# Triangular substitution four columns at a time, and group norms in one stream

## The chip, the cores and the metric

The program runs on one core of a Trainium2 chip. The metric is device time in microseconds (us) of one execution, the median of three. A core has a matrix engine (TensorE, in the views PE, with its weight loads PEld), three engines for elementwise work (VectorE = DVE, ScalarE = ACT, GpSimd = POOL), a queue engine (SyncE = SP) and DMA engines. Every engine runs its own instructions in program order and waits on semaphores for the others.

## What is computed

One layer of a bidirectional backbone on 1024 latent and 128 context tokens, in fp32, model width 1024. The projection w_in feeds two mixers, an RWKV-7 scan in both directions (16 heads of 64) and a gated short convolution; then come the projections w_pa and w_pb, the gated merge, w_o, and a convolutional FFN. Cut to what matters here:

```python
def step(s, inp):                       # the recurrent scan, per direction and head
    r_t, w_t, k_t, v_t, a_t, b_t = inp
    sa = jnp.einsum('bhij,bhj->bhi', s, a_t)
    s = s * w_t[:, :, None, :] + sa[..., None] * b_t[:, :, None, :] + v_t[..., None] * k_t[:, :, None, :]
    return s, jnp.einsum('bhij,bhj->bhi', s, r_t)
...
y = y_f + y_b                           # group norm per head, bonus, gate
o = yn * lp['gn_w'] + lp['gn_b'] + (bonus_f + bonus_b)
...
merged = g_a * (o_a @ lp['w_pa']) + g_b * (o_b @ lp['w_pb'])
x = x + gt1 * (merged @ lp['w_o'])
```

## The kernel before

**Tiles.** The 1152 tokens are processed in three thirds of 384. A dense matrix product runs over weight tiles of 128 output channels; each third takes eight blocks of 128 input channels, and each block three fp32r matmuls (high and low parts of weight and operand), all into the PSUM tile psd. These are the dense matmuls; their operand names the stage: `psd<-h` is w_in, `psd<-x` w_pb and w_pa, `psd<-g` and `psd<-a` the later ones. A weight arrives as wraw by POOL's DMA queue and is split into whi (ACT) and wlo (POOL or DVE).

**The scan in items.** The recurrence is done in chunks of 128 tokens. There are 36 items: four groups of four heads (pp 0 to 3) by nine chunks (n 0 to 8, the last for context), both directions in one item. An item needs *prep* (per pair of heads and third: decays and rates, the matmuls lps), *prep2* (Gram products gpk and gpb on PE, masked into the tiles G, E and O on DVE), the inversion of unit triangular matrices, and the *scan* proper (small matmuls px and py, with DVE work on Wt and Mp between them). After the chunks with n of at least 4 a *finish* runs: group norm, bonus and gate (matmuls fps, six DVE steps for each pair of heads), and a store to OA.

**The inversion.** The 32x32 diagonal blocks are inverted by substitution on DVE (`chain`, L1301 to L1323): Dm holds on each partition the entries of one block, X eight rows of its inverse. For each of 31 columns there is one multiply (`Xt<-X,Dm`) and one add (`X<-X,Xt`), 62 DVE instructions, each dependent on the one before, after each pair a yield. Then four DMAs (`Xd<-X`, ACT's queue) and four more (`G<-Xd`, SP's) bring the blocks back, and `merge` (L1325) joins them with PE (mps).

**The order.** A planner writes the order while the program is built. A clock `clk.now` advances by a fixed cost for each matmul; VectorE, ScalarE and GpSimd have modelled end times. A stream is a generator; it may go on when its own time has come, its condition holds and, where it has a gate, the modelled backlog of DVE and ACT is below it. `drive` alternates one dense matmul with all streams that may go on. The streams of the scan (`start`, L1019) are scan_all, merge_all, vfill_all, prep2_all, load_all, chain_all and prep_all, plus one stream for each finish. So a modelled cost moves the instructions of every engine, and a dense matmul stands between scan work wherever the model has the scan waiting.

**Stages.** While w_in and then w_pb run densely, the streams do the scan beside them. w_pb takes its operand x from OB, split in DVE and ACT instructions at its beginning. Then w_pa takes OA, which every finish must have written; its operand reuses the memory of the scan, as do the 64 wx instructions (L396, 128x1024, the modulation's dot products), placed from the scan's end on. The evacuations are `pbz` for w_pb and `paz`, `mg` for w_pa. w_o and the FFN follow.

Of the kernel before, what the change touches and what calls it, by code (L numbers as in the profile page):

```python
# [8 lines left out]
F32 = mybir.dt.float32  # L9
F32R = mybir.dt.float32r  # L10
AF = mybir.ActivationFunctionType
ALU = mybir.AluOpType
# [3 lines left out]
P = 128  # L16
# [30 lines left out]
class Clock:  # L47


    def __init__(self):  # L50
        self.now = 0.0
        self.e = {"V": 0.0, "A": 0.0, "G": 0.0}
# [24 lines left out]
class Kern:  # L77
# [9 lines left out]
    def mm(self, out, lhsT, rhs, start, stop, cost):  # L87
        self.clk.now += cost
        return self.nc.tensor.matmul(out, lhsT=lhsT, rhs=rhs, start=start, stop=stop)  # L89
# [894 lines left out]
class Scan:  # L984
# [4 lines left out]
    def __init__(self, K, const, apool, par, pc, mask, ident, bones, x0, hw0, hka, oka, dr):  # L989
        self.K, self.nc, self.pc, self.dr = K, K.nc, pc, dr  # L990
        self.mask, self.ident, self.bones, self.x0 = mask, ident, bones, x0
        self.hw0, self.hka, self.oka = hw0, hka, oka
        self.eps = const.tile([P, 1], F32, name="gneps", tag="gneps")
        K.nc.gpsimd.memset(self.eps, GN_EPS)
        self.psx = apool("psx", 1, PSUM)
        self.psy = apool("psy", 1, PSUM)
        self.psm = apool("psm", 3, PSUM)
        self.sets = apool("sets", 3)
        self.one = apool("one", 1)
        self.two = apool("two", 2)  # L1000
        self.ys = apool("ys", 4)
        self.fin = apool("fin", 1)
        self.drp = apool("drp", 2, DRAM)
        nc = K.nc
        self.reset = self.one.tile([P, TH], F32, name="reset", tag="reset")
        nc.gpsimd.memset(self.reset, 1.0)
        nc.gpsimd.memset(self.reset.rearrange("p (c t) -> p c t", t=C)[:, :, 0:1], 0.0)
        self.e65 = self.one.tile([P, 6, C + 1], F32, name="e65", tag="e65")
        nc.gpsimd.memset(self.e65[:, :, 0:1], 1.0)
        self.lwl = self.one.tile([P, 4, P], F32R, name="lwlo", tag="lwlo")  # L1010
        nc.gpsimd.memset(self.lwl[64:128].bitcast(F32), 0.0)
        self.items = [(pp, n) for pp in range(4) for n in range(9)]
        self.info = {}

        self.W = self.one.tile([P, 2, 4, 2, C], F32, name="Wt", tag="Wt")
        self.y, self.PC = {}, {}
        self.NY = 4

    def start(self):  # L1019
        K = self.K  # L1020
# [55 lines left out]
        def scan_all(s):  # L1076
            for i, (pp, n) in enumerate(self.items):
                yield lambda: ("merge", i) in ev and ("prep2", i) in ev
                yield from self.scan(s, i, pp, n)
                ev.add(("scan", i))  # L1080
                if n >= 4:
                    key = 7 - n if n < 8 else 8
                    K.spawn(lambda s2, pp=pp, key=key: self.finish(s2, pp, key), 4, gate=1000, ahead=0)

        K.spawn(scan_all, 0, ahead=0)
        K.spawn(merge_all, 0.5, ahead=0)
        K.spawn(vfill_all, 0.7, ahead=600)
# [213 lines left out]
    def chain(self, s, i):  # L1301


        K = self.K
        inf = self.info[i]
        X, Dm = inf["X"], inf["Dm"]
        tmp = self.one.tile([P, 8, 32], F32, name="Xt", tag="Xt", bufs=2)
        Dv = Dm.rearrange("p (u t) -> p u t", t=32)
        for u in range(31):
            m, n = u // 4 + 1, 31 - u  # L1310
            t_, x_ = tmp[:, 0:m, 0:n], X[:, 0:m, u + 1:32]
            K.tt(s, t_, X[:, 0:m, u:u + 1].to_broadcast([P, m, n]), Dv[:, u:u + 1, u + 1:32].to_broadcast([P, m, n]),
                 ALU.mult)
            K.tt(s, x_, x_, t_, ALU.add)
            s.t = K.clk.e["V"]
            yield
        Xd = self.drp.tile([32, 8, 4, 32], F32, name="Xd", tag="Xd", bufs=4)
        for g in range(4):
            K.dma(Xd[:, :, g, :], X[32 * g:32 * g + 32], "Xw")
        for rb in range(4):  # L1320
            blk = rb % 2
            K.dma(inf["G"][32 * rb:32 * rb + 32, :, 32 * blk:32 * blk + 32],
                  Xd[rb * 8:rb * 8 + 8].rearrange("e m g t -> (m g) e t"), "Xr")  # L1323
# [209 lines left out]
```

## Time and profile before

| | us |
|---|---|
| median of 3 runs | 2983.45 (2982.43 to 2989.89) |
| the profiled execution | 2987.0 |
| its span, first to last instruction | 2985.1 |
| TensorE busy | 2769.4 (93%) |
| VectorE busy | 2012.6 (67%) |
| ScalarE busy | 1267.4 (42%) |
| GpSimd busy | 494.4 (17%) |

Read it so: TensorE is the engine nearest to the span, and its share is an average over stages. From about 330 to 1028 us w_in runs beside preps and the first items; from 1063 to 1740 us w_in runs beside 23 items, one behind another; w_pb runs from 1813 to 1927 us, w_pa to about 2027 us, and the rest is w_o and the FFN. An idle microsecond of an engine costs time only where the end of the program waits for it.

### The profile page before, as it was taken

What the parts mean: (1) busy time and instruction counts of PE and PEld (TensorE: products, weight loads), DVE (VectorE), ACT (ScalarE), POOL (GpSimd) and SP (SyncE); (2) the same over time, 40 slices, a digit from 0 to 9 for tenths busy, and PEclk for the clock granted to TensorE, in tenths of its full rate; (3) what the DMA queues carried; (4) which work ended last, traced back from release to release, by engine and by line L of the source; (5) the groups of instructions that cost most, each with busy time, mean ns of one, the idle gap of its engine ahead of it and who ended that gap; (6) DMA issues with size and microseconds to landing.
All of it is one profiled execution on the core that took longest, in us unless ns stands there. A gap on an engine that the chain in (4) does not pass through costs nothing. (4 is left out here: it accounts for less than half of the span.)

```text
span 2985.1 us, 63295 instructions
## 1 busy us (share of the span) xinstructions
PE 2769.4 (93%) x24762; PEld 2514.1 (84%) x24762; DVE 2012.6 (67%) x5039; ACT 1267.4 (42%) x2544; POOL 494.4 (17%) x678
## 2 busy tenths in 40 slices
PE   7896998999989999889999998999999999999997
PEld 3884887878778777777777788899999999999996
DVE  7457785687667689888887857955555454555556
ACT  4474645555454634334543454123443241424243
POOL 3211121121221111111111112200001101010101
PEclk9997999999999999999999999999999999999998
DMA  4577646466565645545554538843211111111112
GB/s 195 163 238 224 199 148 194 154 175 183 156 185 145 216 109 126 131 109 134 140 139 108 136 115 311 264 141 98 65 43 36 50 40 46 41 41 43 40 44 80
DMA packets 402641, 388.49 MB, mean 130 GB/s; under 512 B 189478, under 2 KB 354214, under 8 KB 402342
## 3 DMA queue, kind: packets, MB, share of 16 engines
q1 hardware_dynamic: 331174, 280.08, 31.1%
q0 software_dynamic: 32000, 99.65, 11.0%
q10 hardware_dynamic: 39168, 4.73, 1.1%
q8 instruction: 195, 3.19, 0.5%
q14 instruction: 104, 0.84, 0.1%
HBM read 268.17 MB, written 116.13 MB: 129 GB/s over the span
## 5 line engine op out<-in xcount | busy, mean ns | idle before, releaser
L89 PE MATMUL psd<-h,whi 128*128 128x384 f32 x3216 | 907.7, 353 | 17.2 <-ACT h L105 9.3
L89 PEld LDWEIGHTS psd<-h,whi 128*128 128x128 f32 x3216 | 591.8, 192 | 52.6 <-issue 12.6
L89 PE MATMUL psd<-h,wlo 128*128 128x384 f32 x1608 | 564.9, 351 | 1.3 <-POOL wlo L110 1.3
L89 PE MATMUL psd<-g,whi 128*128 128x384 f32 (+1 forms) x2112 | 543.2, 338 | 0.0
L105 ACT ACTIVATE whi<-wraw 128x512 fp32r<-128x512 f32 (+2 forms) x334 | 198.3, 594 | 494.3 <-PE psd L89 431.4
L89 PEld LDWEIGHTS psd<-g,whi 128*128 128x128 f32 x2112 | 383.5, 188 | 0.3
L110 POOL TENSOR_TENSOR wlo<-wraw,whi 128x512 fp32r<-128x512 f32 x148 | 199.7, 1350 | 1098.6 <-ACT whi L105 950.9
L89 PE MATMUL psd<-g,wlo 128*128 128x384 f32 (+1 forms) x1056 | 355.9, 337 | 0.0
L89 PEld LDWEIGHTS psd<-h,wlo 128*128 128x128 f32 x1608 | 309.0, 192 | 14.5 <-issue 5.3
L110 DVE TENSOR_TENSOR Xt<-X,Dm 128x60 f32<-128x60 f32 (+24 forms) x1116 | 258.8, 234 | 28.7 <-DMA Dm<-Dd 1.1
L110 DVE TENSOR_TENSOR X<-X,Xt 128x60 f32<-128x60 f32 (+24 forms) x1116 | 253.0, 229 | 27.4 <-DMA O<-fa 0.3
L89 PE MATMUL psd<-a,whi 128*128 128x384 f32 x864 | 218.9, 334 | 0.0
L89 PE MATMUL psd<-x,whi 128*128 128x384 f32 x768 | 200.2, 341 | 10.4 <-ACT x L105 6.7
L89 PEld LDWEIGHTS psd<-g,wlo 128*128 128x128 f32 x1056 | 199.3, 189 | 0.0
L110 DVE TENSOR_TENSOR wlo<-wraw,whi 128x512 fp32r<-128x512 f32 (+2 forms) x186 | 113.7, 611 | 110.6 <-ACT whi L105 110.6
L89 PEld LDWEIGHTS psd<-a,whi 128*128 128x128 f32 x864 | 156.0, 188 | 0.0
L110 DVE TENSOR_TENSOR fu<-psd,rs 128x384 f32<-128x384 f32 x132 | 73.4, 556 | 117.6 <-PE psd L89 105.1
L89 PEld LDWEIGHTS psd<-x,whi 128*128 128x128 f32 x768 | 140.9, 191 | 13.1 <-ACT x L105 7.0
L89 PE MATMUL psd<-a,wlo 128*128 128x384 f32 x432 | 144.0, 334 | 0.0
L122 DVE SCALAR_TENSOR_TENSOR x<-psd,mod,x 128x384 f32<-128x384 f32 (+3 forms) x160 | 79.1, 514 | 94.0 <-PE psd L89 93.9
L105 ACT ACTIVATE BK<-BK,PC 128x128 f32<-128x128 f32 x288 | 94.4, 391 | 108.1 <-PE gpk L89 86.2
L89 PE MATMUL psd<-x,wlo 128*128 128x384 f32 x384 | 130.4, 340 | 4.4 <-DVE wlo L110 4.4
(213 smaller groups left out, 5111.6 us busy)
## 6 DMA issues: line engine op xcount, KB each, us to landing
wraw<-in_w_in POOLq DMA_DIRECT2D x134, 256.0 KB, 3.5
wraw<-in_w_up POOLq DMA_DIRECT2D x88, 256.0 KB, 2.9
llo<-lo SPq DMA_DIRECT2D x98, 192.0 KB, 3.0
BK<-fb SPq DMA_DIRECT2D x36, 512.0 KB, 5.0
Dm<-Dd POOLq DMA_DIRECT2D x144, 128.0 KB, 3.6
wx<-in_wmb SPq DMA_DIRECT2D x32, 512.0 KB, 5.3
fa<-fa SPq DMA_DIRECT2D x40, 384.0 KB, 2.7
fb<-ak SPq DMA_DIRECT2D x40, 384.0 KB, 3.2
```

Of the source, the lines that this page charges most:

```text
L89: return self.nc.tensor.matmul(out, lhsT=lhsT, rhs=rhs, start=start, stop=stop)
L105: self.nc.scalar.activation(out, in_, func, bias=bias, scale=scale)
L110: e.tensor_tensor(out, a, b, op)
L122: self.nc.vector.scalar_tensor_tensor(out, a, sc, b, op0, op1)
```

## The change

In `chain` the columns go four at a time. First the eight 4x4 blocks on the diagonal of each 32x32 block are inverted together into T4 (a copy, a memset, and two pairs of multiply and add). Then for each of the eight groups of four columns the finished columns are multiplied by Dm, and the result by T4. Such a product is one multiply (`Xt<-X,Dm` or `Xt<-X,T4`) into a tile of rows by four columns by terms, and one reduce that sums along the rows (`X<-Xt`). The product with Dm is cut in two parts for the last three groups. That makes 42 DVE instructions per item in place of 62, with nine yields in place of 31; the multiplies take 2384 elements per item, the reduces as many, the inverses of the 4x4 blocks 152. Dm is read with a step of 32 words, T4 with one of 4. Xt and T4 are now single tiles that live as long as the scan, and POOL sets T4's constants at the start. The reduce is charged to the planner by the formula of the multiply.

The second part: the finishes no longer have a stream each. scan_all appends them to a list, and one stream, finish_all, does them one behind another with the same priority and gate.

```diff
--- before.py
+++ after.py
@@ -1009,6 +1009,10 @@
         nc.gpsimd.memset(self.e65[:, :, 0:1], 1.0)
         self.lwl = self.one.tile([P, 4, P], F32R, name="lwlo", tag="lwlo")
         nc.gpsimd.memset(self.lwl[64:128].bitcast(F32), 0.0)
+        self.Xt = self.one.tile([P, 336], F32, name="Xt", tag="Xt")
+        self.T4 = self.one.tile([P, 8, 4, 4], F32, name="T4", tag="T4")
+        nc.gpsimd.memset(self.T4, 0.0)
+        nc.gpsimd.memset(self.T4.rearrange("p j r c -> p j (r c)")[:, :, 0:16:5], 1.0)
         self.items = [(pp, n) for pp in range(4) for n in range(9)]
         self.info = {}
 
@@ -1080,8 +1084,16 @@
                 ev.add(("scan", i))
                 if n >= 4:
                     key = 7 - n if n < 8 else 8
-                    K.spawn(lambda s2, pp=pp, key=key: self.finish(s2, pp, key), 4, gate=1000, ahead=0)
-
+                    self.todo.append((pp, key))
+
+        self.todo = []
+
+        def finish_all(s):
+            for i in range(sum(n >= 4 for _, n in self.items)):
+                yield lambda i=i: len(self.todo) > i
+                yield from self.finish(s, *self.todo[i])
+
+        K.spawn(finish_all, 4, gate=1000, ahead=0)
         K.spawn(scan_all, 0, ahead=0)
         K.spawn(merge_all, 0.5, ahead=0)
         K.spawn(vfill_all, 0.7, ahead=600)
@@ -1304,15 +1316,48 @@
         K = self.K
         inf = self.info[i]
         X, Dm = inf["X"], inf["Dm"]
-        tmp = self.one.tile([P, 8, 32], F32, name="Xt", tag="Xt", bufs=2)
+        tmp, T4 = self.Xt, self.T4
         Dv = Dm.rearrange("p (u t) -> p u t", t=32)
-        for u in range(31):
-            m, n = u // 4 + 1, 31 - u
-            t_, x_ = tmp[:, 0:m, 0:n], X[:, 0:m, u + 1:32]
-            K.tt(s, t_, X[:, 0:m, u:u + 1].to_broadcast([P, m, n]), Dv[:, u:u + 1, u + 1:32].to_broadcast([P, m, n]),
+        cut = lambda *n: tmp[:, :int(np.prod(n))].rearrange(
+            "p (a b c) -> p a b c", b=n[1], c=n[2])
+
+        def times(rows, cols, out, x, d):
+
+            n = (rows, 4, cols)
+            t_ = cut(*n)
+            K.tt(s, t_, x.unsqueeze(2).to_broadcast([P, *n]), d.rearrange("p u c -> p c u").unsqueeze(1).to_broadcast([P, *n]),
                  ALU.mult)
-            K.tt(s, x_, x_, t_, ALU.add)
+            K.nc.vector.tensor_reduce(out, t_, mybir.AxisListType.X, ALU.add)
+            s.use("V", 127 + 1.05 * rows * 4 * cols)
             s.t = K.clk.e["V"]
+
+        def diag(off, n):
+
+            d = Dm[:, off:off + 925:132].unsqueeze(2).to_broadcast([P, 8, n])
+            return bass.AP(d.tensor, d.offset, [*d.ap[:-1], (1, n)])
+
+
+        d = diag(1, 3)
+        K.nc.vector.tensor_copy(T4[:, :, 0:3, 1:4], bass.AP(d.tensor, d.offset, [*d.ap[:-1], (32, 3), (1, 3)]))
+        K.nc.vector.memset(T4.rearrange("p j r c -> p j (r c)")[:, :, 5:11:5], 1.0)
+        s.use("V", 300)
+        for u in range(1, 3):
+            n = (8, u, 3 - u)
+            t_ = cut(*n)
+            dd = diag(33 * u + 1, 3 - u)
+            K.tt(s, t_, T4[:, :, 0:u, u:u + 1].to_broadcast([P, *n]), dd.unsqueeze(2).to_broadcast([P, *n]), ALU.mult)
+            o = T4[:, :, 0:u, u + 1:4]
+            K.tt(s, o, o, t_, ALU.add)
+        s.t = K.clk.e["V"]
+        yield
+
+        for j in range(8):
+            cols = slice(4 * j, 4 * j + 4)
+            h = {5: 2, 6: 3, 7: 3}.get(j, 0)
+            for a, b in ((0, h), (h, j)):
+                if a < b:
+                    times(b - a, 4 * j - 4 * a, X[:, a:b, cols], X[:, a:b, 4 * a:4 * j], Dv[:, 4 * a:4 * j, cols])
+            times(j + 1, 4, X[:, 0:j + 1, cols], X[:, 0:j + 1, cols], T4[:, j])
             yield
         Xd = self.drp.tile([32, 8, 4, 32], F32, name="Xd", tag="Xd", bufs=4)
         for g in range(4):
```

On VectorE, in the middle of a substitution before. Xt, X and Dm are those of the chain; Wt, px, Mp and PC belong to the scan of another item:

```order
L110 TENSOR_TENSOR Xt<-X,Dm 128x6x10
L110 TENSOR_TENSOR Wt<-px,Mp 64x4x64 x2
L110 TENSOR_TENSOR X<-X,Xt 128x6x10
L110 TENSOR_TENSOR Mp<-Wt,PC 64x256 x2
L110 TENSOR_TENSOR Xt<-X,Dm 128x6x9
L110 TENSOR_TENSOR X<-X,Xt 128x6x9
L110 TENSOR_TENSOR Xt<-X,Dm 128x6x8
L110 TENSOR_TENSOR X<-X,Xt 128x6x8
```

On VectorE, in a substitution now, groups five to seven of the columns (T_575 is T4):

```order
L110 TENSOR_TENSOR Xt<-X,T_575 128x80
L1330 TENSOR_REDUCE X<-Xt 128x5x4
L110 TENSOR_TENSOR Xt<-X,Dm 128x160
L1330 TENSOR_REDUCE X<-Xt 128x2x4
L110 TENSOR_TENSOR Xt<-X,Dm 128x144
L1330 TENSOR_REDUCE X<-Xt 128x3x4
L110 TENSOR_TENSOR Xt<-X,T_575 128x96
L1330 TENSOR_REDUCE X<-Xt 128x6x4
L110 TENSOR_TENSOR Xt<-X,Dm 128x288
```

Fewer and longer instructions take the place of the pairs of multiply and add.

On TensorE, around the last group norm (fps) before, and around the last one now. `psd<-h` is a dense matmul of w_in, `psd<-x` one of w_pb:

```order
L89 MATMUL psd<-h_427,wlo 128x384
L89 MATMUL fps<-fb,rb 128x128
L89 MATMUL psd<-h_429,whi 128x384
L89 MATMUL psd<-h_430,whi 128x384
L89 MATMUL psd<-h_429,wlo 128x384
L89 MATMUL psd<-h_431,whi 128x384
L89 MATMUL psd<-h_432,whi 128x384
L89 MATMUL fps<-fb,bones 128x128
L89 MATMUL psd<-h_431,wlo 128x384
```

```order
L89 MATMUL psd<-x_19797,wlo 128x384
L89 MATMUL psd<-x_19776,whi 128x384
L89 MATMUL psd<-x_19777,whi 128x384
L89 MATMUL fps<-fb,rb 128x128
L89 MATMUL psd<-x_19776,wlo 128x384
L89 MATMUL psd<-x_19779,whi 128x384
L89 MATMUL psd<-x_19780,whi 128x384
L89 MATMUL psd<-x_19779,wlo 128x384
L89 MATMUL psd<-x_19782,whi 128x384
L89 MATMUL fps<-fb,bones 128x128
```

The end of the scan has moved from the last matmuls of w_in into w_pb.

On VectorE, in w_pb before (pbz evacuates it; wx and mod are the modulation's dot products):

```order
L122 SCALAR_TENSOR_TENSOR pbz_18198<-pbz_18198,psd_18076 128x384
L396 SCALAR_TENSOR_TENSOR wx_23373,mod_184<-wx_23369,wx_23328 128x1024
L396 SCALAR_TENSOR_TENSOR wx_23377,mod_184<-wx_23375,wx_23327 128x1024
L396 SCALAR_TENSOR_TENSOR wx_23379,mod_184<-wx_23375,wx_23328 128x1024
L122 SCALAR_TENSOR_TENSOR pbz_18291<-pbz_18291,psd_18204 128x384
```

On VectorE, in w_pa now (paz and mg evacuate it):

```order
L122 SCALAR_TENSOR_TENSOR paz_23080<-paz_23080,psd_23055 128x384
L396 SCALAR_TENSOR_TENSOR wx_22675,mod_184<-wx_22671,wx_22576 128x1024
L110 TENSOR_TENSOR paz_23080<-paz_23080,pay_23081 128x384
L110 TENSOR_TENSOR wlo_23102<-wraw_23053,whi_23101 128x512
L396 SCALAR_TENSOR_TENSOR wx_22679,mod_184<-wx_22677,wx_22575 128x1024
L110 TENSOR_TENSOR mg21_23040<-paz_23080,mg20_23039 128x384
L122 SCALAR_TENSOR_TENSOR paz_23117<-paz_23117,psd_23088 128x384
```

Most wx instructions (47 of 64) have moved behind the first evacuation of w_pa.

## Rows read from the trace of the kernel before

**Rows 1.** The page: the span, and the busy time of each engine with its instructions.

```profile
span 2985.1 us, 63295 instructions
...
PE 2769.4 (93%) x24762; PEld 2514.1 (84%) x24762; DVE 2012.6 (67%) x5039; ACT 1267.4 (42%) x2544; POOL 494.4 (17%) x678
```

**Rows 2.** Busy time of each engine in five stretches (window, its length, busy us, instructions).

```profile
330.00:1028.00 698.00, 643.47 (x6278) 567.53 (x6278) 486.16 (x1213) 368.00 (x793) 140.69 (x168) 0.98 0.59 176
1063.00:1740.00 677.00, 619.81 (x9440) 516.28 (x9440) 583.30 (x2096) 274.97 (x624) 118.38 (x173) 0.98 0.49 125
...
1813.00:1927.00 114.00, 106.77 (x590) 104.00 (x590) 101.32 (x163) 23.41 (x48) 28.81 (x29) 0.97 0.87 293
1928.00:2027.00 99.00, 99.00 (x558) 99.00 (x559) 56.81 (x106) 22.20 (x44) 8.58 (x16) 0.98 0.48 144
2200.00:2800.00 600.00, 600.00 (x3432) 599.89 (x3432) 306.46 (x487) 215.32 (x348) 63.30 (x118) 1.00 0.13 42
```

**Rows 3.** The same table for the tile psd alone, so for dense matmuls.

```profile
330.00:1028.00 698.00, 452.02 (x2246) 393.89 (x2244) 16.52 (x30) 39.72 (x88) 0.98 0.59 176
1063.00:1740.00 677.00, 317.70 (x1430) 244.84 (x1430) 9.53 (x18) 20.65 (x42) 0.98 0.49 125
```

**Rows 4.** The page's costliest groups, the two DVE instructions of the substitution.

```profile
L110 DVE TENSOR_TENSOR Xt<-X,Dm 128x60 f32<-128x60 f32 (+24 forms) x1116 | 258.8, 234 | 28.7 <-DMA Dm<-Dd 1.1
L110 DVE TENSOR_TENSOR X<-X,Xt 128x60 f32<-128x60 f32 (+24 forms) x1116 | 253.0, 229 | 27.4 <-DMA O<-fa 0.3
```

**Rows 5.** The tile Xt from 1063 to 1740 us: count, shortest/median/longest ns, first and last start.

```profile
L110 DVE TENSOR_TENSOR Xt<-X,Dm x713: 158/213/1304, 1063.1 to 1737.2; 128x60 f32<-128x60 f32 x16, 128x54 f32<-128x54 f32 x12, 128x66 f32<-128x66 f32 x12, 128x28 f32<-128x28 f32 x10
```

**Rows 6.** DVE groups by shape, whole run: count, busy us, mean ns of one, idle before.

```profile
L110 DVE TENSOR_TENSOR X<-X,Xt 128x8 f32<-128x8 f32 x36 | 7.9, 220 | 0.8
...
L110 DVE TENSOR_TENSOR Xt<-X,Dm 128x30 f32<-128x30 f32 x36 | 6.8, 189 | 0.8
...
L110 DVE TENSOR_TENSOR X<-X,Xt 128x16 f32<-128x16 f32 x36 | 6.3, 175 | 0.9
L110 DVE TENSOR_TENSOR Xt<-X,Dm 128x8 f32<-128x8 f32 x36 | 6.2, 172 | 0.8
...
L396 DVE DVE_READ_ACCUMULATOR wx<-wx 128x1 f32 x64 | 5.2, 81 | 0.0
```

**Rows 7.** DVE in order of time, in the middle of a substitution (start us, us).

```profile
1063.81 0.19 DVE L110 TENSOR_TENSOR X<-X,Xt 128x30 f32<-128x30 f32 x1
1064.03 0.19 DVE L110 TENSOR_TENSOR Xt<-X,Dm 128x29 f32<-128x29 f32 x1
1064.14 0.61 DVE L122 SCALAR_TENSOR_TENSOR cot<-cct,par,cot 128x378 f32<-128x378 f32 x1
```

**Rows 8.** What PE waited for from 1063 to 1740 us: us in total, times, longest.

```profile
PE gpb L89 <- DMA E<-fa: 10.6, 8, 3.4
PE gpk L89 <- DVE G L110: 10.0, 7, 2.4
PE px L89 <- DVE Wt L1387: 9.0, 20, 1.1
```

**Rows 9.** The same waits of PE from 330 to 1028 us.

```profile
PE px L89 <- DVE Wt L1387: 5.0, 8, 2.3
...
PE gpb L89 <- DMA E<-fa: 1.5, 2, 1.1
...
PE gpk L89 <- DVE G L110: 0.9, 2, 0.6
```

**Rows 10.** The tile lps from 330 to 1028 us (the last prep starts at its end).

```profile
L89 PE MATMUL lps<-llo,lwhi x65: 332/392/686, 337.5 to 1026.0; 128*128 128x384 f32 x65
```

**Rows 11.** PE at the first matmul of w_pb (start us, us, idle before).

```profile
1812.87 0.69 PE L89 MATMUL psd<-x,whi 128*128 128x384 f32 x1 [6.65 <-ACT x L105]
```

**Rows 12.** DVE at one evacuation of w_pa (start us, us).

```profile
1932.42 0.55 DVE L122 SCALAR_TENSOR_TENSOR paz<-paz,psd 128x384 f32<-128x384 f32 x1
1932.88 1.22 DVE L396 SCALAR_TENSOR_TENSOR wx<-wx 128x1024 f32<-128x1024 f32 x1
```

## The prediction

> **What bounds the kernel now.** I read the page first. TensorE is busy for 93% of a span of 2985.1 us and VectorE for 67% [rows 1]. An edit on VectorE can therefore save only what PE waits for, so the next view is the busy time by stretch, and the scan alone matters there. In the quiet FFN stretch PE is busy without a gap: 600 us for 3432 dense matmuls, **174.8 ns each** [rows 2]. Beside the scan there are two stretches. From 330 to 1028 us preps, scan items and w_in share the chip; PE is idle for 698.0 − 643.5 = 54.5 us. From 1063 to 1740 us the preps are over and 23 items run one behind the other: 713 of the 1116 multiplies lie there, 713/31 = 23 items, the first at 1063.1 us and the last at 1737.2 us, so one item takes 29.4 us [rows 5]. There VectorE is busy for 583.3 of 677 us, with 2096 instructions, and PE is idle for 57.2 us, 2.5 us per item [rows 2]. The last view is what PE waited for there: operands of the scan's own small matmuls, most of them from VectorE (G, Wt) or through a DMA behind it (E) [rows 8].
>
> An item costs PE about as much in either stretch. Late: 677 − 1430 dense matmuls [rows 3] × 0.1748 = 427 us, over 23 items **18.6 us**, waits included. Early: 698 − 2246 × 0.1748 = 305 us; take off 9 items × 18.6 and 138 us stay for 65 of the 96 lps matmuls, which is 16 of the 24 preps [rows 10], 8.6 us each. If these prices add whatever the order, moving dense matmuls from one stretch to another changes nothing. That is the strongest argument for no change.
>
> **The change: the substitution on VectorE.** Now it takes 258.8 + 253.0 = 511.8 us [rows 4], 14.2 us per item for 62 instructions over 3120 elements. The rows by shape fit 158 ns + 1.05 ns per element: 189 ns at 30, 175 ns at 16 [rows 6]; that gives 9.8 + 3.3 = 13.1 us, so 9% is disturbance. The 16-element shape has rows of two adjacent words and fits the line; the 8-element one has rows of a single word, 32 words apart, and takes 172 ns, (172 − 158)/8 = 1.75 ns per element [rows 6]. (Its twin took 220 ns; I use the lower, less disturbed row.)
>
> The new multiplies read the block's inverse or Dm down a column, so one source hops at every element. Eighteen multiplies over 2384 elements cost 18 × 0.158 + 2384 × 1.75 ns = **7.0 us**; without a price on hopping 5.3, with two passes for each element (2.1 ns) 7.8. I take the row that hops. Eighteen reduces read the same 2384 elements. The trace has no reduce: at the line above 2.8 + 2.5 = **5.3 us**; at least 18 × 81 ns, the shortest VectorE instruction [rows 6], + 2.5 = 4.0; at most, at two passes, 7.8. The six instructions for the 4x4 inverses (72, 16 and four times 16 elements) are some 0.23 + 0.17 + 4 × 0.18 = **1.1 us**. Sum 13.5 us undisturbed, 14.2 to 14.7 with the present disturbance, against 14.2: **a wash**, with ends of 10.4 and 16.7 us undisturbed, −2.7 to +3.6 per item against 13.1.
>
> A rule speaks against the edit. In the rows a single-word hop costs 0.70 ns per element more [rows 6]. The Trainium skill's page "Vector Engine (DVE) Microarchitecture Reference", section "Measured stream behaviour on trn2", gives 1.73 ns per column where one source hops at each element and the full rate for pairs of adjacent words; the rows agree. By either the multiplies come to 7.0 us.
>
> What is left is the hand-over. In the chain an instruction of 0.19 us starts 0.22 us after the one it depends on [rows 7], so twenty fewer save 20 × 0.03 = 0.6 us per item, 14 us over the 23 back-to-back items. But an independent instruction starts inside such a gap [rows 7]; I count half, **−7 us**.
>
> **The change: the order.** By its own formula, 127 + 1.05n for an instruction of n elements, the planner charges 11.1 us for the old substitution and 10.4 for the new, with 9 steps in place of 31, and so re-times everything. I counted dense matmuls ahead of the scan's marks in the order on TensorE. The first merge stands behind 702 of them instead of 798, the last prep behind 3485 instead of 3056, the last merge behind 4951 instead of 4652. Before, 12 items have merged by the last prep, now 22. Dense matmuls per item were 190 early and about 64 late; now they are about 107, 164 and 90 in successive thirds. The last 14 items, with 90 × 0.1748 + 18.6 = 34.3 us each on PE, load VectorE by 583.3/23 = 25.4 us each: 74%, where it was 86%. The 22 beside preps: PE 2783 × 0.1748 + 22 × 18.6 + 20 × 8.6 = 1068 us; VectorE 22 × 25.4 + 20 preps at (486.2 − 9 × 25.4)/16 = 16.1 us = 881 us, 82% [rows 2, 3]. The heaviest load falls from 86 to 82%. What does that save? The three largest waits of PE for VectorE's scan work are 29.6 us late, 1.29 per item [rows 8], and 7.4 us early, 0.82 per item, where VectorE is at 70% [rows 2, 9]: 0.47 us between 86% and 70%. At 74% that gives back 0.35 us for 14 items and at 82% 0.12 for nine, 6 us; I take 0.4 × 23 = **−9 us**, since 393 runs of dense matmuls in place of 514 also spare changes between scan and dense work, which no row prices. Its ends are zero and the whole 57.2 us.
>
> **The ends of the scan.** Before, the scan finished inside w_in. Now the last merge stands some 100 dense matmuls into w_pb, so the 24 splits of w_pb's operand stand on VectorE among the last substitutions. PE already waits 6.65 us there for the first operand [rows 11]. An instruction of about 0.5 us between splits can add at most some sixteen of them, 8 us; I take **+3**. The scan's last group norm stands 300 dense matmuls, 52 us, ahead of w_pa, and OA's loads and splits (24 of 0.55 us on VectorE, 8 DMAs on SP) fit in that; without this cover they would cost some 20 us. finish_all, with its loads and stores on SP, runs items one by one; 300 dense matmuls of slack hide that too. POOL sets three constants once: nothing.
>
> The 64 wx instructions use memory that the scan frees, so they move behind it, 47 of them into w_pa. Per third there are three evacuation steps, 0.47 us from start to start [rows 12], and about two wx of 1.27. VectorE needs 47 × 1.27 + 24 × 1.41 + 10 for weight splits = 104 us, and PE 99.0 [rows 2]: **+4**, with the wx loads on SP now between the loads of the evacuations. w_pb loses them: its window took 114 us for 576 × 0.1748 = 100.7 us of matmuls, 7.2 idle [rows 2]: **−5**.
>
> Sum: 0 − 7 − 9 + 3 + 4 − 5 = **−14 us**. The profiled execution took 2987.0 us (2985.1 in the span and 1.9 around it), the median is 2983.45. Less 14, that is 2973.0 profiled, **2969** on the median's scale.
>
> **Rivals.**
> (1) *Prices add*, as above: neither chain nor order saves. 2983, within 9 us (0.3%, about what a measurement here can tell from no change). For it: 18.6 us per item explains both stretches. Against it: 2.5 us of PE's idle per item is VectorE's doing.
> (2) *Slower: order-coupled stretch.* Ten more items run beside preps, where PE's idle is 54.5/9 = 6.1 us per item against 2.5 without preps. If that is a cost of items and preps mixing, rather than of the preps alone, ten items × 3.6 = +36 us: 2983 + 36 = 3019. It decides from about 1 us per item. For it: the planner believes 10.4 us where I expect 14, so PE arrives early at merges; each substitution step now puts up to six instructions ahead of the short ones (Wt, G) that PE waits for [rows 8]. Against it: VectorE has 18% to spare there.
> (3) *The substitution is dearer*, reduces and hops at two passes: 16.7 us, +3.6 × about 14 items whose pace VectorE sets, less slack, some +20: 3003.
> (4) *It is cheaper*: if hopping in one source costs nothing and hand-overs count whole, 1.7 + 0.6 = 2.3 us per item less, 53 us over 23 items, of which PE's 57.2 us of idle can give back most, some −45: 2938. The Trainium skill's page "VectorE: DVE Perf Modes", section "Rules for kernel authors", advises fewer instructions rather than fewer semaphores, which points this way; no row here has a reduce. The same table calls the reduce the slowest operation, which points to (3).
> That the edit does not do what it says is no case: the order shows 42 instructions.
>
> **Chances.** Forecast 0.36, (1) 0.22, (2) 0.24, (3) 0.08, (4) 0.10. Faster 0.46, within 0.3% 0.22, slower 0.32. The range goes from 2925, most of (4), to 3028, (2) with a quarter on top. The likeliest case's own range is 2950 to 2974.
>
> **What would show it.** Right: a substitution of 13.5 to 14.7 us per item with multiplies of 1.7 ns per element and reduces near 1.05; idle of PE below 2.5 us per item in the late stretch; w_pa near 104 us. Wrong: multiplies or reduces far off these; a stretch beside preps with more than 6 us of idle for each item; the last group norm behind w_pb's end.

## The result and the profile after

The changed kernel takes **3038.16 us** (median of 6, 3028.84 to 3049.97) against 2986.67 us for the kernel before in the same runs (2982.29 to 2992.6): a ratio of 1.0166, 95% interval 1.0138 to 1.0194. It is slower by some 51 us. The forecast was 2969; the range ended at 3028.

The page of the changed kernel, the span and the busy time of each engine (beside [rows 1]):

```profile
span 3038.9 us, 62558 instructions
...
PE 2782.2 (92%) x24762; PEld 2539.9 (84%) x24762; DVE 2030.2 (67%) x4319; ACT 1274.4 (42%) x2551; POOL 494.4 (16%) x680
```

VectorE has 720 instructions fewer, as planned, and is busy for 18 us more. PE is idle for 3038.9 − 2782.2 = 256.7 us where it was 215.7, which is 41 of the 54 us by which the profiled span grew; the other 13 are in PE's busy time, at a mean granted clock of 0.957 where it was 0.975.

Where it happens is read from busy time by stage. The first table is of the kernel before, cut at the last prep, the first matmul of w_pb, its last evacuation, w_pa's last evacuation and the end (window, its length, busy us with instructions for PE, PEld, DVE, ACT and POOL, then the granted clock, the DMA share and GB/s):

```profile
250.00:1026.00 776.00, 700.80 (x6743) 614.99 (x6741) 550.92 (x1435) 406.53 (x875) 158.75 (x194) 0.96 0.59 177
1026.00:1813.00 787.00, 717.19 (x10520) 603.68 (x10518) 647.32 (x2260) 328.72 (x732) 138.51 (x197) 0.98 0.50 133
1813.00:1929.00 116.00, 107.84 (x594) 105.07 (x595) 103.32 (x168) 23.41 (x48) 29.34 (x30) 0.97 0.87 292
1929.00:2028.00 99.00, 99.00 (x562) 99.00 (x561) 56.31 (x111) 22.68 (x46) 8.58 (x16) 0.99 0.48 145
2028.00:2985.00 957.00, 940.52 (x5346) 932.62 (x5344) 508.09 (x835) 349.05 (x581) 100.69 (x174) 0.99 0.16 50
```

The same five stages of the changed kernel:

```profile
250.00:1322.00 1072.00, 949.56 (x10770) 826.22 (x10770) 810.09 (x1889) 523.79 (x1136) 202.67 (x260) 0.93 0.56 159
1322.00:1829.00 507.00, 450.90 (x6025) 397.60 (x6023) 360.19 (x950) 192.22 (x416) 95.38 (x128) 0.95 0.44 119
1829.00:1981.00 152.00, 137.99 (x1057) 126.12 (x1058) 104.94 (x214) 50.84 (x110) 28.57 (x34) 0.96 0.65 214
1981.00:2084.00 103.00, 101.88 (x576) 101.24 (x575) 100.31 (x189) 21.34 (x39) 8.58 (x16) 0.99 0.78 253
2084.00:3039.00 955.00, 937.45 (x5333) 930.02 (x5331) 508.55 (x845) 349.13 (x587) 100.67 (x174) 0.99 0.16 50
```

From w_pa's end on the two agree (957 and 955 us), and w_pa itself takes 103 us for 99, as the sum had it. Everything else is lost between 250 us and the last evacuation of w_pb: 776 + 787 + 116 = 1679 us before, 1072 + 507 + 152 = 1731 now. PE's idle there rose from 75 + 70 + 8 = 153 us to 122 + 56 + 14 = 192. VectorE's load over the two stages of the scan did *not* rise: it was 551 + 647 = 1198 of 1563 us (77%) and is 810 + 360 = 1170 of 1579 us (74%). Beside the preps it went from 71 to 76%, afterwards from 82 to 71%. PE waits more for an engine that is, on the average, less loaded.

The substitution itself came out as costed. VectorE's groups by shape in the changed kernel (count, busy us, mean ns of one; T is T4), beside [rows 6]:

```profile
L110 DVE TENSOR_TENSOR Xt<-X,Dm 128x256 f32<-128x256 f32 x72 | 48.2, 669 | 1.7
...
L110 DVE TENSOR_TENSOR Xt<-X,Dm 128x336 f32<-128x336 f32 x36 | 27.9, 774 | 0.9
...
L1330 DVE TENSOR_REDUCE X<-Xt 128x12 f32<-128x336 f32 x36 | 17.9, 498 | 0.8
...
L110 DVE TENSOR_TENSOR Xt<-X,T 128x128 f32<-128x128 f32 x36 | 13.6, 379 | 0.7
```

The multiply of 336 elements takes 774 ns, (774 − 158)/336 = 1.83 ns per element, that of 256 (669 − 158)/256 = 2.0; the forecast took 1.75 from the one row that hops. The product with T4, which steps by 4 words, takes (379 − 158)/128 = 1.73 at 128 elements, the lowest of its eight shapes. The reduce of 336 takes 498 ns, 1.01 ns per element, the line of a plain multiply. All the substitution's groups sum to 516 us, 14.3 us per item; it was 511.8 [rows 4]. Of the 14.3 the multiplies take 8.1 us, the reduces 5.2 and the 4x4 inverses 1.05.

What is new is a wait. Of PE's waits from 250 to 1830 us in the kernel before, here is one of the Gram products, for the load of their operand BK, and the two largest ahead of the merges' matmuls (mps):

```profile
PE gpb L89 <- DMA BK<-fb: 6.5, 3, 3.9
...
PE mps L89 <- DVE Xt L110: 3.3, 3, 2.6
...
PE mps L89 <- DVE RSt L1330: 1.8, 2, 1.4
```

In the changed kernel, with the two largest other waits:

```profile
PE mps L89 <- DVE RSt L1375: 47.8, 20, 5.1
PE gpb L89 <- DMA BK<-fb: 23.0, 15, 4.0
PE gpk L89 <- DVE G L110: 21.4, 13, 4.0
```

So a second wait grew, by 16.5 us, and it is for a DMA; what lies behind it is not shown. One of the twenty before mps, in order of time. On PE the last dense matmul before it, and the merge's first:

```profile
1632.61 0.34 PE L89 MATMUL psd<-h,wlo 128*128 128x384 f32 x1
1638.02 0.81 PE L89 MATMUL mps<-RSt,G 32*32 32x32 f32 x23 [5.07 <-DVE RSt L1375]
```

The merge waits for RSt, VectorE's transpose of G. The four DMAs that bring the blocks of this item into G are issued here, on SP's queue:

```profile
1629.48 1.80 SPq L128 DMA_DIRECT2D G<-Xd  x4
```

Their size and median time from issue to landing, from 1620 to 1645 us:

```profile
G<-Xd SPq DMA_DIRECT2D x4, 32.0 KB, 1.8
```

And on VectorE: the end of this item's substitution, the beginning of the next, and the transpose among its last products:

```profile
1625.17 0.29 DVE L1330 TENSOR_REDUCE X<-Xt 128x32 f32<-128x128 f32 x1
1625.38 0.19 DVE L1341 COPY T<-Dm 128x72 f32<-128x72 f32 x1
...
1637.25 0.27 DVE L1330 TENSOR_REDUCE X<-Xt 128x28 f32<-128x112 f32 x1
1637.43 0.43 DVE L1375 STREAM_TRANSPOSE RSt<-G 128x256 f32<-128x256 f32 x1
```

The item's blocks had left VectorE at 1625.5 us, and their DMAs were issued by 1631.3. But the next substitution begins in the same instant and holds VectorE until 1637.25, twelve microseconds with scarcely a gap, and the transpose stands behind most of it. PE, which needs 0.4 us of VectorE, waits 5.07. By an estimate from the last issue and the median landing the blocks lay in G at about 1633.1, so some 4 us of this wait are VectorE's queue.

The granted clock is lower where the holes are. Four windows of 50 us around this place and another such hole (4.46 us at 1565 us):

```profile
1500.00:1550.00 50.00, 46.99 (x747) 40.49 (x748) 35.80 (x86) 19.07 (x45) 8.26 (x14) 1.00 0.62 159
1550.00:1600.00 50.00, 41.13 (x601) 33.81 (x599) 32.20 (x83) 16.51 (x38) 5.67 (x8) 0.83 0.35 87
1600.00:1650.00 50.00, 43.44 (x499) 39.94 (x498) 38.94 (x106) 16.21 (x35) 10.91 (x13) 0.90 0.42 113
1650.00:1700.00 50.00, 45.69 (x521) 40.05 (x517) 32.82 (x82) 20.38 (x42) 9.55 (x12) 1.00 0.43 115
```

PE is busy for 41.1 and 43.4 us of the middle two, and the granted clock is 0.83 and 0.90 of full speed there, a mix of its two levels, 2.4 and 1.2 GHz; with 47.0 and 45.7 us busy it is 1.00.

### The profile page after: what moved, and what is told of

The parts are those of the page before. It is cut to its first block, busy times and chain, and to the rows that moved or that the text cites. A ratio compares the mean times of both kernels' runs of the same rounds, so it can differ in the third digit from the quotient of the medians.

```text
span 3038.9 us, 62558 instructions
## 1 busy us (share of the span) xinstructions
PE 2782.2 (92%) x24762; PEld 2539.9 (84%) x24762; DVE 2030.2 (67%) x4319; ACT 1274.4 (42%) x2551; POOL 494.4 (16%) x680
## 5 line engine op out<-in xcount | busy, mean ns | idle before, releaser
L89 PE MATMUL psd<-h,whi 128*128 128x384 f32 x3216 | 897.9, 354 | 18.0 <-ACT h L105 9.2
L89 PEld LDWEIGHTS psd<-h,whi 128*128 128x128 f32 x3216 | 600.7, 195 | 43.5 <-ACT h L105 10.2
L89 PEld LDWEIGHTS psd<-h,wlo 128*128 128x128 f32 x1608 | 313.3, 195 | 14.2 <-POOL wlo L110 5.8
L1330 DVE TENSOR_REDUCE X<-Xt 128x12 f32<-128x144 f32 (+13 forms) x648 | 186.8, 288 | 17.1
L110 DVE TENSOR_TENSOR Xt<-X,Dm 128x16 f32<-128x16 f32 (+4 forms) x360 | 188.3, 523 | 9.4
L105 ACT ACTIVATE BK<-BK,PC 128x128 f32<-128x128 f32 x288 | 98.2, 393 | 100.7 <-PE gpk L89 84.4
```

The lines of the kernel that those rows point to most:

```text
L105: self.nc.scalar.activation(out, in_, func, bias=bias, scale=scale)
L110: e.tensor_tensor(out, a, b, op)
L1330: K.nc.vector.tensor_reduce(out, t_, mybir.AxisListType.X, ALU.add)
```

## The experiments

All runs were compared with the kernel before on the same chip; its medians in the five sets of runs lie between 2986 and 2990 us, so medians of different sets compare to some 4 us. In the planner's own time a substitution is planned 39 us long in the kernel before, from its first step to its modelled end, and 26 us in the changed kernel; this is called its planned length. The 39 is a mean: about 48 us for the items beside the preps and 35 for those behind.

### Instructions and order, one at a time

`old_clock` (the planner's clock, not TensorE's): the new instructions, the old charges.

```diff
-            s.use("V", 127 + 1.05 * rows * 4 * cols)      # and the other charges of the new chain
+        def charge(us):
+            for u in us:
+                n = (u // 4 + 1) * (31 - u)
+                s.use("V", 127 + 1.05 * n)
+                s.use("V", 127 + 1.05 * n)
+                s.t = K.clk.e["V"]
+                yield
...
+            yield from charge(range(4 * j, min(4 * j + 4, 31)))
```

> The new 42 instructions of the substitution and the one stream of group norms, but the planner is charged the old 31 steps with their old costs, so that the order is nearly that of before (11 of 36 merges ahead of the last prep, as before; 525 runs of dense matmuls, 514 before). Theory A (the loss is in the order that the new costs and yields make, above all merges that PE reaches too early): 2987 us within 10, the substitution 14.3 us per item as in the changed kernel. Theory B (the new instructions themselves, hopping multiplies and reduces, hold VectorE up): 3020 us or more, since they are all here.

Measured 2996.77 us, ratio 1.0029 (1.0016 to 1.0043). Page, and PE's wait before the merges:

```profile
span 2994.5 us, 62590 instructions
...
PE 2776.4 (93%) x24762; PEld 2517.9 (84%) x24762; DVE 2028.5 (68%) x4319; ACT 1264.7 (42%) x2540; POOL 494.5 (17%) x680
```

```profile
PE mps L89 <- DVE RSt L1378: 2.2, 3, 1.0
```

`new_clock_old_chain`: the old 62 instructions in nine steps, charged like the new ones.

```diff
+        for j in range(8):
+            for u in range(4 * j, min(4 * j + 4, 31)):
+                ...                                        # the old multiply and add, not charged
+            for rows, cols in parts:
+                for _ in range(2):
+                    s.use("V", 127 + 1.05 * rows * 4 * cols)
+                s.t = K.clk.e["V"]
+            yield
```

> The old 62 instructions of the substitution, but the planner is charged the new 9 steps with their new costs, so that the order is like that of the changed kernel (22 merges ahead of the last prep). Theory A: slow, 3025 to 3050 us, with PE waiting at the merges for the transpose RSt some 40 us. Theory B: about 2987 us, since the new instructions are absent.

Measured 3031.66 us, ratio 1.0145 (1.0108 to 1.0181). PE's waits before the merges:

```profile
PE mps L89 <- DVE RSt L1349: 22.9, 13, 3.2
...
PE mps L89 <- DVE X L1328: 13.5, 5, 5.9
```

So the order made by the new charges and steps costs 42 us with the old instructions and 41 us (3038 − 2997) with the new; the instructions in the old order cost some 9. Theory B, that the instructions alone do it, falls. With the old instructions part of the loss lies elsewhere, though: the scan ends later, and the stretch behind w_pa takes 978 us for 957 (below, at `paced_early`). Up to w_pb's last evacuation the order alone costs 15 us, the instructions alone 9, and the two together 52 (the table below). So in the scan it is the pair that costs: a short plan with instructions that need more.

The second part of the change, finish_all, moves nothing by itself: put into the kernel before, it leaves the positions of the scan's matmuls among the dense ones where they were. It was not run alone.

### The hop, and the merge's margin

`no_hop`: the changed kernel, reading along rows. It leaves out the turn that the substitution needs, so what it computes is not the inverse.

```diff
-            K.tt(s, t_, ..., d.rearrange("p u c -> p c u").unsqueeze(1).to_broadcast([P, *n]),
+            K.tt(s, t_, ..., d.unsqueeze(1).to_broadcast([P, *n]),
...
-                    times(..., Dv[:, 4 * a:4 * j, cols])
+                    times(..., Dv[:, cols, 4 * a:4 * j])
```

> The changed kernel in its own order, but the multiplies read Dm and T4 along rows instead of down columns, so that no source hops (the inverses are then not the right ones; work and order are the same). Multiplies should fall from about 2.0 to 1.05 ns per element, some 2.3 us per item of 14.3. Theory A: part of the waiting at the merges goes, 3038 to about 3015 us, and the rest stays. Theory B: most of the loss goes, 2990 us.

Measured 2979.26 us, ratio 0.9965 (0.9944 to 0.9987): faster than before, and 59 us faster than the changed kernel, with its order. The page, and two of the multiplies:

```profile
span 2977.2 us, 62558 instructions
...
PE 2753.7 (92%) x24762; PEld 2515.2 (84%) x24762; DVE 1967.1 (66%) x4319; ACT 1275.0 (43%) x2551; POOL 491.4 (17%) x680
```

```profile
L110 DVE TENSOR_TENSOR Xt<-X,Dm 128x256 f32<-128x256 f32 x72 | 36.9, 513 | 1.7
...
L110 DVE TENSOR_TENSOR Xt<-X,Dm 128x336 f32<-128x336 f32 x36 | 19.8, 549 | 0.9
```

The substitution takes 451 us in all, 65 less. Nearly every microsecond of that came back, and more than the expectation of either theory: in this order VectorE's time in the substitution counts almost in full although VectorE is idle for a quarter of the stretch. Half of the gain, 28.5 us, is in PE's busy time (2782.2 to 2753.7) at a clock of 0.967 for 0.957, half in its idle. PE's wait for BK stays (22.4 us).

The Trainium skill's page "Vector Engine (DVE) Microarchitecture Reference", section "Measured stream behaviour on trn2", has 1.73 ns per column for one source that hops 4 KiB at each element, against 1.05 for contiguous ones. The rows here, with steps of 32 words, come out alike: 774 and 549 ns at 336 elements, 0.67 ns per element apart.

`margin`: one number.

```diff
-                s.t = K.clk.now + 5000
+                s.t = K.clk.now + 9000
```

> The changed kernel with one number altered: the merge is planned 9000 instead of 5000 ns after the modelled end of its substitution. Nothing else is added or taken away. Theory A in the form that the merges are the place: PE's 48 us of waiting before mps go nearly, 2995 to 3005 us. If the loss is spread over the order (VectorE's backlog beside preps, group norms, clock): 3025 to 3040 us although that wait goes. Theory B: 3038 us.

Measured 3029.19 us, ratio 1.0130 (1.0092 to 1.0167).

```profile
PE mps L89 <- DVE RSt L1375: 39.5, 13, 7.7
```

The later plan for the merges gets back 9 us, but the wait falls only from 47.8 to 39.5 us. So a larger margin does not take the wait away, and this run does not tell what the wait is worth; `paced_700` below does. PE is busy for 2756.8 us here at a clock of 0.960, 25 us less than in the changed kernel, and idle for 276.8, 20 us more.

### Honest charges, and the hop taken away for real

`honest`: a multiply and its reduce together are charged what the chip takes for them.

```diff
-            s.use("V", 127 + 1.05 * rows * 4 * cols)
+            s.use("V", 189 + 1.95 * rows * 4 * cols)
```

> The changed kernel's instructions and steps; only the planner's charge for a reduce is raised, so that a multiply with its reduce is charged 316 + 3.0 ns per element, what the trace of the changed kernel shows for the two together. Theory A (a planner that believes a shorter substitution than the chip runs lets PE arrive early): the order slackens, 3005 to 3020 us. Theory C (what costs is that the steps are 9 in place of 31, whatever they are charged, so that a substitution no longer stands behind the other streams' backlog 31 times): little changes, 3025 to 3040 us.

Measured 3030.98 us, ratio 1.0151 (1.0123 to 1.0178), planned length 29 us.

```profile
PE mps L89 <- DVE RSt L1375: 46.6, 13, 6.1
```

That is in theory C's range. But the honest charge lengthens the plan by 3 us only, so this run does not part the number of steps (C) from missing room; `paced`, with nine steps and more room, does, and against C.

`turned`: ScalarE turns Dm, so that no multiply hops and the inverses are the right ones.

```diff
+                yield lambda: i == 0 or ("chain", i - 1) in ev
+                inf["DT"] = self.one.tile([P, 31, 31], F32, name="DT", tag="DT")
+                K.act(s, inf["DT"], inf["Dm"].rearrange("p (u t) -> p t u", t=32)[:, 1:32, 0:31], AF.Copy)
...
-        Dm = self.one.tile([P, 1024], F32, name="Dm", tag="Dm", bufs=2)
+        Dm = self.one.tile([P, 1024], F32, name="Dm", tag="Dm", bufs=1)
```

> The changed kernel, but ScalarE copies each item's Dm once into a turned tile (31 x 31 words), and T4 is built turned, so that no multiply hops; one buffer for Dm and one for the turned tile in place of two for Dm, so that the copy of an item waits for the substitution before it. The result is the right one. If the hopping multiplies on VectorE are what the new order has no room for, as the run without hops says: 2975 to 2995 us. If the copy on ScalarE (some 1 to 2 us per item) and its hand-over take the place of the hop: 3010 to 3040 us.

Measured 3026.85 us, ratio 1.0140 (1.0110 to 1.0171). In the short order the hop's time does not come back, although the substitution takes 442 us as in the next run. VectorE's wait for the copy, from 250 to 1830 us:

```profile
DVE T L1347 <- ACT DT L105: 50.8, 25, 9.9
```

It waits for the copy ahead of 25 of the 36 substitutions; whether ScalarE, the hand-over or the single buffer makes the copy late, this run does not tell.

`turned_old_clock`: the turned copy with the old charges (the edits of `turned` and `old_clock` together).

> The turned copy as above, with the planner charged the old 31 steps and costs (the order nearly that of before). If in the old order VectorE has room, as the run with the old clock and the hops says, taking the hops away gives little: 2983 to 2995 us. If a microsecond of the substitution counts in any order: 2940 to 2960 us.

Measured **2962.91 us**, ratio 0.9928 (0.9903 to 0.9954), faster than both kernels. ScalarE's copy (shortest/median/longest ns), and a multiply:

```profile
L105 ACT ACTIVATE DT<-Dm x36: 1854/1926/2020, 261.5 to 1697.7; 128x961 f32<-128x961 f32 x36
```

```profile
L1334 DVE TENSOR_TENSOR Xt<-X,DT 128x256 f32<-128x256 f32 x72 | 31.6, 439 | 1.4
```

The multiply of 256 elements takes 439 ns for 669. The gain over `old_clock` is 34 us, or 30 when each is set against the kernel before in its own runs; I had expected 2 to 14, since VectorE has room in the old order. The substitution is 61 us shorter (442 for 503), so about half of that came back: VectorE has room there for the other half.

`turned_margin`: the edits of `turned` and `margin` together, the margin at 7500.

> The turned copy in the new order with the merge planned 7500 instead of 5000 ns after the modelled end of its substitution. If merges that come early still cost PE some 28 us, as in the run without hops, this is the fastest: 2955 to 2975 us. If other waits take their place, as in the run with the margin alone: within 10 us of the turned copy alone.

Measured 3010.24 us, ratio 1.0083 (1.0057 to 1.0110): 17 us better than `turned`, outside both of the expected ranges.

### Room between the steps

The steps of the substitution end later in the planner's time, by a pause; instructions and charges are those of the changed kernel.

```diff
-        s.t = K.clk.e["V"]
+        s.t = K.clk.e["V"] + 1500          # 700 and 3000 in the other two
         yield
...
+            s.t = K.clk.e["V"] + 1500
             yield
```

> The changed kernel; the only edit is that each of the nine planned steps of a substitution ends 700 ns later in the planner's time, so that one is planned 31 us long from its first step to its end (26 us in the changed kernel, 39 before). 23 merges stand ahead of the last prep, as in the changed kernel (22). Theory S (what went is the slack between the planned and the real substitution): about half the loss comes back, 3010 to 3022 us. Theory M (what costs is that some 22 items in place of 11 run beside preps): nothing comes back, 3028 to 3045 us.

Measured 3027.62 us, ratio 1.0132 (1.0102 to 1.0163), between the two ranges and next to theory M's. The wait before the merges, with the largest one now; in the changed kernel this one came to 1.9 us:

```profile
PE gpb L89 <- DMA E<-fa: 25.6, 14, 4.3
...
PE mps L89 <- DVE RSt L1376: 16.1, 8, 6.1
```

> The same with 1500 ns: 36 us planned, near the 39 of before, but still 19 merges ahead of the last prep. This run tells the two apart best. Theory S: 2990 to 3005 us, PE's waits before mps under 15 us. Theory M: 3015 to 3035 us.

Measured 3003.49 us, ratio 1.0041 (1.0020 to 1.0063), in theory S's range.

```profile
PE mps L89 <- DVE RSt L1376: 11.1, 6, 5.0
```

> The same with 3000 ns: 45 us planned and 12 merges ahead of the last prep, as before. Theory S and theory M: 2985 to 3003 us, as with the old clock. If it is neither (31 small steps matter as such): above 3015 us.

Measured 3012.52 us (2998.79 to 3014.61), ratio 1.0069 (1.0042 to 1.0095); its profiled execution, with a span of 2996.8 us, lies at the lower end of that. The median is above both theories' range and below the 3015 us of the third.

`turned_paced`, the pause of 1500 on the turned copy:

> The turned copy (no hops) with 1500 ns per step: 36 us planned, 17 merges ahead of the last prep. Theory S: within 10 us of the turned copy in the old order, 2955 to 2973 us. Theory M: 2985 to 3010 us.

Measured 2978.52 us (2966.19 to 2992.51), ratio 0.9969 (0.9945 to 0.9993), between the two ranges and nearer to theory S's. Without the pause it was 3027.

Room between planned steps gives back 35 of 51 us, with 19 items beside preps. But in `paced_700` the wait before the merges falls from 48 to 16 us and the time only by 11: that wait is a symptom, and when it goes others stand in its place, here the one for E. Left were two readings: the items beside preps (theory M) or the missing room in every substitution (theory S).

```diff
+            s.t = K.clk.e["V"] + (3000 if ("prep", NPAIR - 1, 1) not in K.events else 0)    # paced_early
+            s.t = K.clk.e["V"] + (0 if ("prep", NPAIR - 1, 1) not in K.events else 3000)    # paced_late
```

> The changed kernel with 3000 ns pauses between the planned steps of a substitution as long as preps are left, and none afterwards: 12 merges ahead of the last prep, as before, then 24 items planned as short as in the changed kernel (23 us). Theory M (the loss belongs to items beside preps): 2990 to 3005 us. Theory S (slack is missing in every item): 24 of 36 items lack it, 3015 to 3030 us.

Measured 3047.32 us, ratio 1.0200 (1.0174 to 1.0225), above both ranges. The stretch beside the preps (250 to 1036 us), the rest of the scan and w_pb, and PE's largest wait after w_pa:

```profile
250.00:1036.00 786.00, 695.48 (x6873) 610.56 (x6872) 565.76 (x1242) 402.83 (x872) 155.16 (x190) 0.96 0.59 174
1036.00:1960.00 924.00, 826.78 (x10945) 718.88 (x10944) 658.23 (x1756) 327.68 (x739) 168.53 (x229) 0.94 0.48 127
```

```profile
PE psd L89 <- DVE x L122: 18.9, 1, 18.9
```

> The reverse: no pause while preps are left, so 22 merges ahead of the last prep as in the changed kernel, and 3000 ns pauses for the last 14 items. Theory M: nothing comes back, 3028 to 3045 us. Theory S: 22 of 36 items lack slack, 3010 to 3025 us.

Measured 3020.24 us, ratio 1.0095 (1.0062 to 1.0128), in theory S's range.

> The turned copy (no hops) with the pauses only beside preps: 11 merges ahead of the last prep. Theory M: about the turned copy in the old order, 2955 to 2970 us. Theory S: 2990 to 3005 us, since the turned copy without pauses took 3027.

Measured 3014.92 us, ratio 1.0085 (1.0056 to 1.0115), 10 us above theory S's range and 45 above theory M's.

Theory M falls: with only 12 items beside the preps and 786 us for them (776 before), `paced_early` is the slowest of all. A part of its loss lies behind the scan: the scan ends so late in w_pb that the wx work is late and PE waits 18.9 us for x behind w_pa. `new_clock_old_chain` has the same wait:

```profile
PE psd L89 <- DVE x L122: 18.4, 1, 18.4
```

To keep that apart, here is each profiled execution by the starts of the last evacuations of w_pb and w_pa (from the groups of pbz and paz) and its span, in us:

| kernel | planned length | last pbz | to last paz | to the end | median |
|---|---|---|---|---|---|
| before | 39 | 1928.9 | 99.1 | 957.1 | 2986.67 |
| old_clock | 39 | 1937.7 | 99.9 | 956.9 | 2996.77 |
| paced_3000 | 45 | 1939.4 | 100.5 | 956.9 | 3012.52 |
| paced | 36 | 1945.6 | 100.6 | 957.0 | 3003.49 |
| paced_early | 48, then 23 | 1959.5 | 113.4 | 977.9 | 3047.32 |
| paced_late | 27, then 45 | 1962.1 | 99.0 | 957.4 | 3020.24 |
| paced_700 | 31 | 1963.9 | 100.7 | 958.0 | 3027.62 |
| honest | 29 | 1974.8 | 98.8 | 957.0 | 3030.98 |
| changed kernel | 26 | 1981.1 | 102.6 | 955.2 | 3038.16 |
| new_clock_old_chain | 26 | 1944.0 | 104.6 | 978.3 | 3031.66 |

The rows are of one execution each; that of `paced_3000` is its fastest, 14 us below its median, and executions of the changed kernel lie up to 21 us apart, so neighbouring rows are not told apart. In the large, the rows with the new instructions, from `old_clock` to the changed kernel, are in the order of the room: 45 to 36 us planned end within 8 us of one another (within 16 by the medians), and 31, 29 and 26 us lie 26, 37 and 43 us behind `old_clock`. Without room in 22 or in 24 of 36 items the loss is 24 and 22 us, wherever those items lie. `paced_early` plans the items beside the preps as the kernel before does, and only the later ones short (23 us for some 35). The turned copies fall in line: their last pbz starts at 1902.8 us with the old charges, 1933.0 with the pause, 1955.8 with the pause beside preps only, 1969.1 without. So theory S is the one that fits the scan, though five of the seven runs with pauses lie outside the range that it gave. `paced_early` and `new_clock_old_chain` lose a further 21 us behind w_pa, and 14 and 5 us in it, with their scan's end so late in w_pb; the forecast of theory S for `paced_early` had not foreseen that.

## Why the prediction was wrong

**The substitution: right.** A wash was forecast, 14.2 to 14.7 us per item; it is 14.3, with hops of 1.8 to 2.0 and reduces at 1.0 ns per element. Undisturbed, the multiplies were put at 7.0 us and took 8.1; the reduces (5.3) and the 4x4 inverses (1.1) came out.

**The hand-overs, −7: not seen.** In nearly the old order the new instructions keep VectorE in the substitution 9 us less (503 for 512 [rows 4]) and the kernel is 9 us slower. Why is open; the two orders are not quite the same.

**The order, −9: the step that failed.** The sum took PE's waits to follow VectorE's average load, whose higher value was to fall from 86 to 82%. The load did fall (by the stages above the higher value went from 82 to 76%), and PE's idle rose by 39 us. What PE waits for is not a share but a queue: short instructions behind the next substitution on an engine that works in order. That the planned length fell from 39 to 26 us could have been read from the planner. That its charges were short of the chip's stood in rival (2) and not in the sum; by `honest` they are worth 7 us of the loss. I counted dense matmuls per item and did not ask what stood ahead of each short instruction. With the new instructions the order costs 41 us where the sum had −9.

**The ends.** w_pa took 103 us, forecast 104. At w_pb's start PE waited 1.06 and 4.76 us in the place of the single 6.65 [rows 11]; +3 was too dear, and the −5 for w_pb cannot be found, since the end of the scan now lies in it and its window went from 116 to 152 us:

```profile
1829.22 0.86 PE L89 MATMUL psd<-x,whi 128*128 128x384 f32 x2 [1.06 <-ACT x L105]
1834.84 0.69 PE L89 MATMUL psd<-x,whi 128*128 128x384 f32 x1 [4.76 <-DVE x L110]
```

The group norms ended within w_pb, as forecast; where the scan ended later still, the price of some 20 us for a lost cover was the right size (21), but by luck: it fell on the wx work and not on OA.

**The rivals.** Rival (2) had the sign and most of the size, 3019, and one sentence of it names what the timeline shows: steps that put up to six instructions ahead of the short ones that PE waits for. Its price rested on items beside preps, and `paced_early` refutes that; its doubt, that VectorE has 18% to spare, is the same error as in the sum. Rival (4) was wrong: the hop is not free. Where `no_hop` takes it away the new order pays, but with 2979 us, 10 below its own runs of the kernel before, not with 2938. Rival (3) had the sign, but the substitution is no dearer than before (14.3 us per item). Rival (1), that prices add in any order, is wrong: the order alone moved the time by 41 us.

**The signs.** PE's idle in the late stage was to stay below 2.5 us per item and is 56/14 = 4.0, so that sign of being right failed. Beside the preps it is 122/22 = 5.6, below the 6 that was to show the sum wrong: that sign was set too high.

**The range** was too short on the side of rival (2): a quarter on top of 36 us was no bound, since the whole stretch is coupled to the order, and the granted clock fell with it (0.93 and 0.95 in the two stages, for 0.96 and 0.98), which no term carried.

**What stays open** is how the loss is shared between the waits, and why 45 us of planned length is no better than 36. That VectorE's backlog counts is shown by runs that shorten or spread it; but the pauses move all other work too, PE's wait for BK is no wait for VectorE, and the single waits were not taken away one by one.

## What to carry to other kernels

When a planner writes the order from modelled costs, an edit that shortens a planned task moves everything, and the room that the longer plan left may have been doing work: run the new instructions with the old charges, and the old instructions with the new ones, before judging either. An average load below 80% said nothing here about short instructions that stand behind a long dependent chain on an engine that works in order; look what stands ahead of each one that another engine waits for. A source read down a column cost 1.8 to 2.0 ns per element on VectorE here, against 1.05 along rows in the line of the kernel before; turned once on another engine, and with the old order kept, the same substitution made this kernel faster (2963 us).

## What the hardware showed unexpectedly

A reduce along rows costs no more per element than a plain multiply (1.01 ns at 336 elements). ScalarE's copy that reads with a step of 32 words takes 1.93 us for 961 elements, 2.0 ns per element, so turning is not free there either. What PE's idle costs beyond its own length stays open: from the changed kernel to `no_hop` 33 us less idle came with 28.5 us less busy time, at a granted clock of 0.967 for 0.957, but in `margin` 20 us more idle came with 25 us less busy time, at 0.960.
